# An encoder layer on one core: v from the scaled raw input, its rms applied after the products, its shift added behind attention

## The chip, the core and the metric

The kernel runs on one core of a Trainium2 chip. Its engines work side by side and are ordered by semaphores alone: TensorE (PE, with its weight loads as PEld), VectorE (DVE), ScalarE (ACT), GpSimd (POOL) and SyncE (SP), which issues nearly all transfers. The metric is the time of one execution in microseconds (us); every time below is in us unless it says ns.

## The reference

One layer, 512 tokens of width 1024, all fp32. What matters here:

```python
mod = silu(c) @ w_c + b_c
shift, scl, gate = split(mod, 3)
h = rms_norm(x, g_pre) * (1 + scl) + shift
xa, za, q, k, v, zb, ga, gb = split(h @ w_in, 8)      # 1024 columns each
y_a = ((scan_fwd(conv(xa)) + scan_bwd(conv(xa))) * silu(za)) @ w_pa
y_b = (neighbourhood_attention(q, k, v) * silu(zb)) @ w_pb   # softmax over 8x16 keys, 16 heads of 64
x = x + gate * ((sigmoid(ga) * y_a + sigmoid(gb) * y_b) @ w_o)
out = rms_norm(x, g_final)
```

rms_norm divides a token's row by its root mean square; the softmax weights of one query add up to one.

## The kernel before

Each fp32 product is three fp32r products: an operand is split into a rounded high part and the rest (hi and lo; L380 casts on ACT, L383 subtracts on DVE or GpSimd), and mm3 (L388) adds hi*hi, hi*lo and lo*hi. Width 1024 is 8 blocks k of 128 rows; the normalised input stands transposed, as hh[k] and hl[k], 128 channels by 512 tokens.

The order of every engine's instructions is fixed ahead by a planner (Plan, L101). Each op has an engine or two, a cost, a rank and its data; the planner plays time forward by these costs and gives an engine the op of lowest rank among those that can begin next. HEAD (L44) overrides ranks by name for the start of the kernel. The hardware then runs each engine's list in that order, and an instruction that must wait holds up all behind it on its engine. lock=True marks DVE ops that the planner keeps apart from GpSimd's. SBUF buffers are slots of 512 columns (T, 36 of them) and 1024 columns (W, 32), PSUM is 8 banks of 512 columns given out by class (B, LIMITS). Loads are issued on SP, at most 8 in flight, each waiting for the landing of the one eight before it.

The start runs as follows. par, a table of vectors with c in its first 8 rows, is loaded by ACT's queue (L405). ACT and DVE make silu(c) (L409, L412), TensorE transposes par into prm (L415) and spreads silu(c) over all partitions into two banks cbs (L434 to L440); ACT copies these to SBUF as silr. DVE makes mods from prm (L422). x comes transposed in 8 loads (L474). ACT squares it, DVE adds the squares up, TensorE sums over partitions (L496), ACT and DVE take the root (rstd_ops, L454), TensorE spreads the result over partitions (rb, L509), and ACT copies it (rbs). modulate (L535) makes one column each of scale and shift of block k: DVE multiplies 128x1024 weights wc by silu(c) and sums; for block 0's scale TensorE does it. make_h (L577) is then ht = x * scale * rms on DVE, hh = ht + shift on ACT and hl on DVE. split_v (L604) splits the weights of v.

The first products (vmm, L636) are v: 8 units (2 halves of the columns by 4 tiles of 128 tokens), one bank each, all of them walking over k together, 3 products per unit and block. Stand-in products (fill, L502) keep TensorE running before. vout (L668) copies v to DRAM scratch as hi and lo parts. Then follow 72 projections (proj, L691) of 24 products each, numbered from 9: for each of 4 groups q, k and z of two head pairs, with scores, softmax (attend, L805) and the products with v between the products of the next projections. At the end of attend the gate sz is multiplied by the softmax's reciprocal rcx (L909) and by the head pair's output yt (L911). Then the recurrent branch, the gates, and w_o with the final norm.

## Time and profile before

| | us |
|---|---|
| median of 3 runs (558.74 to 559.42) | 558.84 |
| span of the profiled execution | 556.9 |
| TensorE busy in it | 548.6 (99%) |
| DVE, ACT, GpSimd busy | 388.4, 320.1, 102.1 |

The profile is of one execution; its span runs from the first to the last instruction, and the time of a run has about 2 us more around it. Engine rows give start, duration and shape; an idle time and its releaser stand in brackets where the engine waited. A matmul's duration includes its way through the array, so consecutive ones overlap in the timeline; the chain counts each from the end of the one before.

### The profile page before, as it was taken

What the parts mean: (1) busy time and instruction counts of PE and PEld (TensorE: products, weight loads), DVE (VectorE), ACT (ScalarE), POOL (GpSimd) and SP (SyncE); (2) the same over time, 40 slices, a digit from 0 to 9 for tenths busy, and PEclk for the clock granted to TensorE, in tenths of its full rate; (3) what the DMA queues carried; (4) which work ended last, traced back from release to release, by engine and by line L of the source; (5) the groups of instructions that cost most, each with busy time, mean ns of one, the idle gap of its engine ahead of it and who ended that gap; (6) DMA issues with size and microseconds to landing.
All of it is one profiled execution on the core that took longest, in us unless ns stands there. A gap on an engine that the chain in (4) does not pass through costs nothing.

```text
span 556.9 us, 7643 instructions
## 1 busy us (share of the span) xinstructions
PE 548.6 (99%) x2769; PEld 458.8 (82%) x2769; DVE 388.4 (70%) x707; ACT 320.1 (57%) x557; POOL 102.1 (18%) x98
## 2 busy tenths in 40 slices
PE   8999999999999999999999999999999999999995
PEld 8788888888888888888887888888788888888884
DVE  5999733775775785897458958867968973569423
ACT  6442624763763863766986984996698242223242
POOL 0102757546546520000000000000000000000220
PEclk9999999999999999999999999999999999999998
DMA  8993895651551563035244035131239322480002
GB/s 294 408 408 124 299 302 198 155 191 54 148 202 67 123 200 114 4 95 190 78 123 159 31 122 167 41 114 62 89 100 376 130 76 75 152 301 1 0 38 115
DMA packets 30825, 82.54 MB, mean 148 GB/s; under 512 B 4548, under 2 KB 5700, under 8 KB 30788
## 3 DMA queue, kind: packets, MB, share of 16 engines
q1 hardware_dynamic: 30500, 81.73, 43.3%
q8 instruction: 22, 0.36, 0.3%
q10 hardware_dynamic: 288, 0.33, 0.2%
q14 instruction: 15, 0.12, 0.1%
HBM read 75.60 MB, written 6.44 MB: 147 GB/s over the span
## 4 chain that ended last, share of the span: by engine, by line
PE 99%; DVE 0%; POOL 0%; issue 0%; ACT 0%; POOLq 0%
PE acc L386 79%; PE hx L386 8%; PE pv L386 3%; PE pt L848 2%; PE sp L386 2%; PE gt L386 2%; PE hx L504 1%; PE hx L437 1%; PE hd L551 0%; PE hd L496 0%; PE hd L513 0%; DVE yo L1215 0%; DVE yo L1183 0%; DVE xr L1187 0%; ACT sd L1205 0%
## 5 line engine op out<-in xcount | busy, mean ns | idle before, releaser
L386 PE MATMUL acc<-hhl,whi 128*128 128x512 f32 x784 | 243.1, 391 | 0.0
L386 PEld LDWEIGHTS acc<-hhl,whi 128*128 128x128 f32 x784 | 145.7, 188 | 29.2
L386 PE MATMUL acc<-hhl,wlo 128*128 128x512 f32 x392 | 152.9, 390 | 0.0
L386 PEld LDWEIGHTS acc<-hhl,wlo 128*128 128x128 f32 x392 | 73.6, 188 | 15.5
L380 ACT CAST whi<-wraw 128x1024 fp32r<-128x1024 f32 x72 | 74.4, 1045 | 1.8 <-DMA wraw<-in_w_in_dram 0.9
L1194 POOL TENSOR_TENSOR yo<-yo,gfin 128x512 f32<-128x512 f32 x6 | 8.1, 1350 | 337.8 <-ACT xr L1191 337.7
L383 POOL TENSOR_TENSOR wlo<-wraw,whi 128x1024 fp32r<-128x1024 f32 x23 | 56.0, 2438 | 64.0 <-ACT whi L380 32.1
L383 DVE TENSOR_TENSOR wlo<-wraw,whi 128x1024 fp32r<-128x1024 f32 x49 | 59.2, 1220 | 2.3 <-ACT whi L380 2.1
L386 PE MATMUL acc<-woh,mhl 128*128 128x512 f32 (+1 forms) x144 | 40.4, 366 | 0.0
L386 PE MATMUL acc<-ybhl,whi 128*128 128x512 f32 x128 | 39.4, 390 | 0.0
L386 PE MATMUL acc<-yahl,whi 128*128 128x512 f32 x128 | 39.4, 390 | 0.0
L738 POOL TENSOR_TENSOR nb<-msk,braw 128x192 f32<-128x192 f32 (+1 forms) x48 | 30.7, 670 | 27.8 <-DMA braw<-in_rpb_dram 26.7
L837 ACT ACTIVATE p<-p,mn 128x192 f32<-128x192 f32 (+1 forms) x64 | 30.4, 478 | 6.7 <-DVE mn L830 6.6
L1079 DVE SCALAR_TENSOR_TENSOR gm<-gm,acc 128x512 f32<-128x512 f32 x16 | 11.0, 688 | 33.0 <-PE acc L386 33.0
L386 PE MATMUL hx<-vh,hhl 128*128 128x512 f32 x112 | 33.5, 389 | 0.0
L830 DVE CUSTOM_DVE_ANT_0 p<-sp,nb 128x192 f32<-128x192 f32 (+1 forms) x64 | 31.4, 602 | 0.6 <-PE sp L386 0.2
L386 PEld LDWEIGHTS acc<-woh,mhl 128*128 128x128 f32 x144 | 26.1, 189 | 4.4
L985 DVE SCALAR_TENSOR_TENSOR xc<-acc,prm,xc 128x511 f32<-128x511 f32 (+1 forms) x24 | 18.0, 750 | 14.9 <-ACT xc L978 14.3
L386 PEld LDWEIGHTS acc<-ybhl,whi 128*128 128x128 f32 x128 | 24.0, 188 | 5.0
L386 PEld LDWEIGHTS acc<-yahl,whi 128*128 128x128 f32 x128 | 24.0, 188 | 5.0
L386 PE MATMUL acc<-wol,mhl 128*128 128x512 f32 (+1 forms) x72 | 26.4, 366 | 0.0
L386 PE MATMUL acc<-yahl,wlo 128*128 128x512 f32 x64 | 24.9, 390 | 0.0
(195 smaller groups left out, 939.5 us busy)
## 6 DMA issues: line engine op xcount, KB each, us to landing
wraw<-in_w_in_dram SPq DMA_DIRECT2D x56, 512.0 KB, 5.0
wc<-in_w_m_dram SPq DMA_DIRECT2D x22, 512.0 KB, 10.1
vt<-vscr SPq DMA_DIRECT2D x20, 256.0 KB, 3.5
vscr<-va SPq DMA_DIRECT2D x8, 512.0 KB, 4.3
wraw<-in_w_pb_dram SPq DMA_DIRECT2D x8, 512.0 KB, 3.5
wraw<-in_w_pa_dram SPq DMA_DIRECT2D x8, 512.0 KB
wo<-in_w_o_dram SPq DMA_DIRECT2D x8, 512.0 KB, 5.2
wv<-in_w_v_dram SPq DMA_DIRECT2D x7, 512.0 KB
```

The source lines that it names most:

```text
L380: return lambda e: nc.scalar.copy(o(), i()) if e == "ACT" else nc.vector.tensor_copy(o(), i())
L383: return lambda e: ENGINE[e].tensor_tensor(o(), a(), b().bitcast(F32), op=ALU.subtract)
L386: nc.tensor.matmul(o, a, b, start=first, stop=last)
L437: nc.tensor.matmul(cb.ap[:, k * P:(k + 1) * P], ident.ap[:, 4 * n + k:4 * n + k + 1].to_broadcast([P, P]), par_sb.ap, start=True, stop=True)
L504: op("PE", 0.3, lambda e: nc.tensor.matmul(wb.ap[:, :P], onesc.ap, onesc.ap, start=True, stop=True), 5000 + j, r=[onesc], hold=[wb], until ...
L738: nc.gpsimd.tensor_tensor(o, mv, view, op=ALU.subtract)
L830: nc.vector.tensor_tensor_reduce(out=o, in0=v(spv(h, e)[:, :nk]), in1=v(nb[:, h, :nk]), scale=1.0, scalar=3e38, op0=ALU.add, op1=ALU.min, ...
L837: nc.scalar.activation(pv2(i), pv2(i), AF.Exp, bias=mn.ap[:, c:c + 1], scale=-1.0, accum_out=sm.ap[:, 4 * h + b:4 * h + b + 1])
L848: nc.tensor.transpose(ptp.ap[:, j * P:(j + 1) * P], pt_.ap[:, j * P:(j + 1) * P], ident.ap)
L985: nc.vector.scalar_tensor_tensor(a, b, wcol, a, op0=ALU.mult, op1=ALU.add)
L1079: op("DVE", dve(512), lambda e: nc.vector.scalar_tensor_tensor(t.ap, t.ap, 1.0, o.ap, op0=ALU.add, op1=ALU.mult), n - 1.9, r=[o], rw=[t], ...
L1194: op(("DVE", "POOL"), (dve(w), pool_(w)), lambda e: ENGINE[e].tensor_tensor(y(), y(), gfin[n].ap[:, gs], op=ALU.mult), rank + 0.1, r=[gfin ...
```

## The change

v is linear in h, so v = rms * ((x * scale) @ W_v) + shift @ W_v, and a softmax's weights add up to one, so the second part is a constant per channel that can be added to attention's output. The change uses both:

- hx[k], lx[k]: raw x times the scale of block k, split, made from the first loads; v's products take these. rms multiplies in vout (voh, vol), per token.
- rms comes from x loaded a third time, in token rows (xn), squared with a running sum on ACT; TensorE spreads it (rb) into one bank, ACT copies (rbs).
- Five units of v walk over k together; the other three follow one after the other. At most 6 banks for v; the 2 banks of silu(c) (pair) are read by all modulations directly and given back after silr is copied.
- c is loaded once more by itself (c8), ahead of par; silu(c) is spread from 8 rows. Block 0's scale is made on DVE.
- h for the other projections is made later: ht on GpSimd, shift on ACT (hs), cast (hh) on ACT, hl on DVE. All shift columns (wc*0) are loaded after the rest.
- shift is turned to a row through DRAM and spread (shr); per head pair DVE multiplies the transposed weights of v (w_vt, 8 new loads of 512 KB) by it and sums (cv). L909 and L911 become ytr and yb.
- x and the weights of v come in loads of 512 KB; HEAD has new ranks. The loads of the start, by rank: wc01, x0, wv0, x1, wc11, wc21, wv1, wc31, wv2, wv3, wv4, x2, wv5, wc41, wc51, wv6, wc61, xn1, xn2, x3, wc71, wv7, xn3, xn0, then the shifts; w9 to w15 (projection weights) come in between as their gates open.

```diff
-LIMITS = {"hx": 8, "acc": 3, "sp": 8, "pt": 2, "pv": 2, "mi": 2, "hd": 3, "gt": 8}
+LIMITS = {"cb": 2, "hx": 6, "acc": 3, "sp": 8, "pt": 2, "pv": 2, "mi": 2, "hd": 3, "gt": 8}
...
+    "rn": -24.5555, "sq3": -24.3814, "rd": -24.3812, "sq1": -24.3808, "rbs": -23.8168, "sq0": -23.8167,
+    "sq2": -23.7377, "rr": -23.1868, "rv": -23.1868, "rb": -20.771, "par": -19.6461, "c8": -19.4661,
+    "wc01": -18.9967, "mod011": -18.2714, "x0": -18.0591, "wv0": -18.0187, "x1": -17.8175, "wc11": -17.7222,
+    "cb0": -17.5889, "cb1": -17.5886, "wc21": -17.0274, "wv1": -17.0273, "vl20": -16.9829, "lx5": -16.8171,
+    "vl40": -16.6325, "vl11": -16.2216, "wc31": -16.2215, "vl00": -15.9897, "mod010": -15.9895, "vh00": -15.2342,
+    "wv2": -15.2275, "wv3": -15.2144, "wv4": -15.0849, "vh21": -14.965, "vh31": -14.9648, "hx0": -14.9556,
+    "vh11": -14.9227, "hx1": -14.8864, "vh10": -14.7844, "x2": -14.7206, "vh01": -14.4144, "wv5": -14.1437,
+    "hx2": -14.1283, "wc41": -11.2127, "wc51": -10.9689, "mod10": -10.9101, "lx2": -10.6732, "vl30": -10.6506,
+    "lx3": -10.6502, "lx0": -10.6498, "vl10": -10.6494, "mod41": -10.6491, "mod30": -10.649, "vl61": -10.649,
+    "mod11": -10.6328, "vl21": -10.6163, "wv6": -10.4746, "mod61": -10.4424, "wc61": -9.9113, "xn1": -9.9112,
+    "vol": -9.8476, "xn2": -9.7211, "w9": -9.2629, "voh": -9.1099, "vh50": -9.1099, "vh61": -8.6009,
+    "mod21": -8.5472, "vl41": -8.5331, "vl51": -8.5327, "x3": -8.496, "wc71": -8.4249, "lx1": -8.3181,
+    "vl70": -8.318, "mod51": -8.3178, "vl50": -8.3178, "vl71": -8.3176, "vl31": -8.2434, "hx6": -8.2376,
+    "vl60": -7.9836, "vh40": -7.456, "hx4": -7.3237, "mod20": -7.1116, "vh20": -6.9125, "hx7": -6.9125,
+    "sht": -6.8405, "vl01": -6.8401, "lx4": -6.6641, "lx7": -6.664, "hx3": -6.547, "vh41": -6.5466, "hx5": -6.5327,
+    "vh51": -6.5326, "vh71": -6.449, "vh60": -6.4007, "mod71": -6.1288, "mod00": -6.1285, "wv7": -5.9891,
+    "vh30": -5.87, "vh70": -5.6813, "xn3": -5.5188, "lx6": -4.8536, "w10": -4.518, "mod31": -4.4195, "xn0": -4.3793,
+    "wc60": -3.8783, "wc30": -3.7292, "wc40": -3.5764, "wc50": -3.1556, "wc10": -3.0913, "wc20": -2.8982,
+    "wc00": -2.1309, "w11": -1.8085, "wc70": -1.3694, "wlo10": 3.5288, "ht0": 4.0245, "hs3": 4.37, "ht6": 4.3831,
+    "ht1": 4.5527, "ht2": 4.5848, "wlo11": 4.5852, "ht5": 4.9249, "whi9": 4.9984, "ht7": 5.2332, "ht3": 5.3297,
+    "ht4": 5.3298, "hh3": 5.3561, "hh2": 5.3603, "hh1": 5.473, "hs5": 5.4732, "hh4": 5.4799, "silr": 5.5365,
...
+}
+AFTER = []
...
+    def bank(i, cls):
+        if cls == "cb":
+            assert i not in plain
+            twin.append(i)
+            return pair[:, 512 * len(twin) - 512:512 * len(twin)]
+        if i not in twin:
+            plain.add(i)
+            return ps.tile([P, 512], F32, tag=f"b{i}", name=nm(cls))
+        if not rest:
+            first.close()
+            rest.append(ctx.enter_context(tc.tile_pool(name="pr", bufs=1, space=bass.MemoryType.PSUM)))
+        return rest[0].tile([P, 512], F32, tag=f"b{i}", name=nm(cls))
+
...
+    tan8, c8 = const("tan8", [8, P]), const("c8", [8, P])
+    op("ACT", 0.45, lambda e: nc.scalar.dma_start(c8.ap, par[:8, :]), -41, w=[c8], late=2.6, name="c8")
+    op("ACT", 0.45, lambda e: nc.scalar.dma_start(par_sb.ap, par), -40, w=[par_sb], late=3.3, name="par")
+    op("ACT", 0.3, lambda e: nc.scalar.activation(tan8.ap, c8.ap, AF.Tanh, scale=0.5), -25, r=[c8], w=[tan8])
+    op("DVE", 0.3, lambda e: nc.vector.scalar_tensor_tensor(c8.ap, tan8.ap, 1.0, c8.ap, op0=ALU.add, op1=ALU.mult),
+       -22, r=[tan8], rw=[c8])
...
+    cbs = [B("cb") for _ in range(2)]
+        def f(e, n=n):
+                nc.tensor.matmul(cbs[n].ap[:, k * P:(k + 1) * P], ident.ap[:8, 4 * n + k:4 * n + k + 1].to_broadcast([8, P]), c8.ap,
+        op("PE", 0.6, f, -21 + n, r=[ident, c8], w=[cbs[n]], name=f"cb{n}")
...
+    for j in range(4):
+        load(xT[j], whole(xT[j]), x_t[j], -19.9 + 0.1 * j, 524288, spare=2, name=f"x{j}")
+    ssx, rxc = const("ssx", [P, NT]), const("rxc", [P, NT])
+    for t in range(NT):
+        xn = W("xn")
+        load(xn, whole(xn), x[t * P:(t + 1) * P, :], 0, 524288, spare=2, name=f"xn{t}")
+        op("ACT", act(1024, 0, True), lambda e, xn=xn, t=t: nc.scalar.activation(xn.ap, xn.ap, AF.Square, accum_out=ssx.ap[:, t:t + 1]), 0,
+           rw=[xn], w=[ssx], name=f"sq{t}")
...
+    op("ACT", 0.29, lambda e: nc.scalar.activation(rsd.ap, ssx.ap, AF.Sqrt, bias=epsc.ap), 0, r=[ssx, epsc], w=[rsd], name="rd")
+    op("DVE", 0.17, lambda e: nc.vector.tensor_scalar(rv.ap, ssx.ap, D * EPS, None, op0=ALU.add), 0, r=[ssx], w=[rv], name="rv")
+    op("DVE", 0.17, lambda e: nc.vector.reciprocal(rrc.ap, rsd.ap), 0, r=[rsd], w=[rrc], name="rr")
+    op("DVE", 0.57, newton, 0, r=[rrc, rv], w=[rq, rxc], lock=True, name="rn")
...
+    rb, rbs = B("mi"), T("rbs")
+    def spread(e):
+        for t in range(NT):
+            nc.tensor.matmul(rb.ap[:, t * P:(t + 1) * P], rxc.ap[:, t:t + 1].to_broadcast([P, P]), ident.ap, start=True, stop=True)
+    op("PE", 0.5, spread, -12, r=[rxc, ident], w=[rb], name="rb")
+    spread_done = op("ACT", act(512), cast(whole(rbs), whole(rb)), -12, r=[rb], w=[rbs], name="rbs")
...
+    def modulate(k, m):
+        t, r = W("wc"), C("sc", 1, 10) if m else shc.part(k, k + 1)
+        (scs if m else shs)[k] = r
+        b = mods.ap[:, 8 + k:9 + k] if m else pc(16 + k, 17 + k)
+        g = mods.ap[:, k:k + 1] if m else 0.5
+        load(t, whole(t), w_m[3 * k + m], k - 5, 524288, spare=2, name=f"wc{k}{m}")
...
+                op("DVE", dve(512) + 0.08, lambda e, j=j, z=z: nc.vector.tensor_tensor_reduce(
+                    out=t.ap[:, z], in0=t.ap[:, z], in1=cbs[j].ap, scale=g, scalar=a.ap if j else b, op0=ALU.mult, op1=ALU.add,
+                    accum_out=r.ap if j else a.ap), -0.5, r=[cbs[j], mods, prm] + [a] * j, rw=[t], w=[r if j else a], name=f"mod{k}{m}{j}")
+            return
+        op("DVE", dve(1024) + 0.08, lambda e: nc.vector.tensor_tensor_reduce(
+            out=t.ap, in0=t.ap, in1=pair, scale=g, scalar=b, op0=ALU.mult, op1=ALU.add, accum_out=r.ap),
+           k - 1.5, r=cbs + [mods, prm], rw=[t], w=[r], after=[zero], name=f"mod{k}{m}")
+    def split_x(k):
+        hx[k], lx[k] = two("xhl")
+        xk = lambda: xT[k // 2].ap[:, k % 2 * 512:k % 2 * 512 + 512]
+        op("ACT", act(512, 1), lambda e: nc.scalar.activation(hx[k].ap, xk(), AF.Copy, scale=scs[k].ap), k - 1.19,
+           r=[xT[k // 2], scs[k]], w=[hx[k]], name=f"hx{k}")
+        op("DVE", dve(512) + 0.06, lambda e: nc.vector.scalar_tensor_tensor(
+            lx[k].ap, xk(), scs[k].ap, hx[k].ap.bitcast(F32), op0=ALU.mult, op1=ALU.subtract), k - 1.18,
+           r=[xT[k // 2], hx[k], scs[k]], w=[lx[k]], lock=True, name=f"lx{k}")
...
+        xk = lambda: xT[k // 2].ap[:, k % 2 * 512:k % 2 * 512 + 512]
+        op("POOL", pool_(512), lambda e: nc.gpsimd.tensor_tensor(t.ap, xk(), rbs.ap, op=ALU.mult), k - 1.2, r=[xT[k // 2], rbs], w=[t], name=f"ht{k}")
+        op("ACT", act(512, 2), lambda e: nc.scalar.activation(t.ap, t.ap, AF.Identity, scale=scs[k].ap, bias=shs[k].ap), k - 1.195,
+           r=[scs[k], shs[k]], rw=[t], name=f"hs{k}")
+        op("ACT", act(512), cast(whole(hh[k]), whole(t)), k - 1.19, r=[t], w=[hh[k]], name=f"hh{k}")
+        op("DVE", dve(512), sub(whole(hl[k]), whole(t), whole(hh[k])), k - 1.18, r=[t, hh[k]], w=[hl[k]], lock=True, wait=1.45, name=f"hl{k}")
...
+        t, z = W("wv"), (slice(0, S), slice(S, D))
+        load(t, whole(t), w_v[k], k - 4.5, 524288, spare=2, name=f"wv{k}")
+        (h0, l0), h1, l1 = two("vhl"), T("vh", F32R), T("vl", F32R)
+        for n, hi, lo in ((0, h0, l0), (1, h1, l1)):
+            vh[k, n], vl[k, n] = (hi, whole(hi)), (lo, whole(lo))
+            op("ACT", act(512), lambda e, hi=hi, n=n: nc.scalar.copy(hi.ap, t.ap[:, z[n]]), k - 1.1, r=[t], w=[hi], name=f"vh{k}{n}")
+            op(*(("POOL", pool_(512)) if k and n else (("DVE", "POOL"), (dve(512), pool_(512)))), sub(whole(lo), lambda n=n: t.ap[:, z[n]], whole(hi)), k - 1.09, r=[t, hi],
+               w=[lo], lock=True, name=f"vl{k}{n}")
...
+        modulate(k, 1)
+        split_x(k)
+        split_v(k)
+    for k in range(KD):
+        modulate(k, 0)
+    silr = W("silr")
+    op("ACT", act(1024), cast(whole(silr), lambda: pair), 9, r=cbs, w=[silr], name="silr")
...
+        for j, parts in enumerate(([0], [1], [2]) if k < 2 else ([0, 1], [2]) if k < KD - 1 else ([0, 1, 2],)):
+            for m, u in enumerate(VU[:5]):
+                ops.append(vmm(u, k, parts, k + 0.1 * j + 0.01 * m))
+            fill(ops[4], vps[VU[4]])
+    for m, u in enumerate(VU[5:]):
+        ops = [vmm(u, k, [0, 1, 2], 8 + 0.2 * m + 0.01 * k) for k in range(KD)]
...
+        rs = rxc.ap[:, t:t + 1]
+        op("ACT", act(512, 1), lambda e: nc.scalar.activation(view(0, 192), src(), AF.Copy, scale=rs), rank, r=[vps[u], rxc], w=[a], name="voh")
+        def low(e):
+            for b in range(2):
+                o, i1 = (a.ap.rearrange("p (g c) -> p g c", g=4)[:, :, c:c + 64] for c in (64 + 64 * b, 192 * b))
+                nc.vector.scalar_tensor_tensor(o, src()[:, :, b, :], rs, i1.bitcast(F32), op0=ALU.mult, op1=ALU.subtract)
+        op("DVE", 2 * dve(256), low, rank, r=[vps[u], rxc], rw=[a], name="vol")
...
+    sscr = pl.fixed(dp.tile([32, P], F32, name="sscr"))
+    op("DVE", 0.2, lambda e: nc.vector.transpose(sht.ap[:, :32], shc.ap), 7, r=[shc], w=[sht], name="sht")
+    op("SP", 0.5, lambda e: nc.sync.dma_start(turned(sscr.ap), sht.ap[:, :32]), 8, r=[sht], w=[sscr], size=16384, late=SLACK, name="shs")
+    shr = W("shr")
+    load(shr, whole(shr), bass.AP(sscr.ap.tensor, sscr.ap.offset, [[0, P], [1, D]]), 8, 524288, r=[sscr], spare=3, name="shr")
...
+    def v_bias(pr, rank, after):
+        t = W("wvt")
+        load(t, whole(t), w_vt[pr], rank - 2, 524288, after=after, spare=5, name="wvt")
+        op("DVE", dve(1024) + 0.08, lambda e: nc.vector.tensor_tensor_reduce(
+            out=t.ap, in0=t.ap, in1=shr.ap, scale=0.5, scalar=0.0, op0=ALU.mult, op1=ALU.add, accum_out=cvs[pr].ap), rank,
+           r=[shr], rw=[t], w=[cvs[pr]], lock=True, name="cv")
...
-        op("DVE", dve(512), lambda e: nc.vector.tensor_tensor(rbc(sz.ap), rbc(sz.ap), nat(rcx.ap), op=ALU.mult),
-           pos - 0.3, r=[rcx], rw=[sz], lock=True, name="szr")
-        op("DVE", dve(512), lambda e: nc.vector.tensor_tensor(rbc(sz.ap), nat(yt.ap), rbc(sz.ap), op=ALU.mult), pos + 0.5, r=[yt],
-           rw=[sz], lock=True, name="yb")
+        v_bias(pr, pos + 0.2, gate_of(len(main), 2))
+        op("DVE", dve(512), lambda e: nc.vector.tensor_tensor(rbc(rct.ap), nat(yt.ap), nat(rcx.ap), op=ALU.mult),
+           pos + 0.4, r=[yt, rcx], rw=[rct], lock=True, name="ytr")
+        op("DVE", dve(512), lambda e: nc.vector.scalar_tensor_tensor(sz.ap, rct.ap, cvs[pr].ap, sz.ap, op0=ALU.add, op1=ALU.mult),
+           pos + 0.5, r=[rct, cvs[pr]], rw=[sz], lock=True, name="yb")
```

## Rows read from the trace of the kernel before

**Rows 1.** Page, chain that ended last: share of the span by engine.

```profile
PE 99%; DVE 0%; POOL 0%; issue 0%; ACT 0%; POOLq 0%
```

**Rows 2.** That chain in order of time: start us, us, engine, tile, line, count.

```profile
1.51 3.36 PE hx L504 x14
...
5.09 2.99 PE hx L437 x16
8.08 2.46 PE hx L504 x22
...
16.34 44.23 PE hx L386 x192
60.57 32.64 PE acc L386 x144
...
550.14 0.43 DVE yo L1183
```

**Rows 3.** Timeline of DVE, 0 to 62 us: start us, us, instruction [idle before].

```profile
4.29 0.28 DVE L412 SCALAR_TENSOR_TENSOR par_sb<-tan,par_sb 8x128 f32<-8x128 f32 x1 [4.29 <-ACT tan L409]
...
5.86 0.17 DVE L425 TENSOR_SCALAR mods<-mods 128x8 f32<-128x8 f32 x1
...
14.89 0.16 DVE L462 SCALAR_TENSOR_TENSOR rx<-q,r 128x2 f32<-128x2 f32 x1
14.99 0.48 DVE L584 SCALAR_TENSOR_TENSOR ht<-xT,sc,hd 128x256 f32<-128x256 f32 x1
...
17.92 0.81 DVE L566 CUSTOM_DVE_ANT_0 wc<-wc,hx,mods 128x512 f32<-128x512 f32 x1 [0.31 <-DMA wc<-in_w_m_dram]
...
24.51 1.34 DVE L571 CUSTOM_DVE_ANT_0 wc<-wc,silr,mods 128x1024 f32<-128x1024 f32 x1
...
37.68 0.75 DVE L600 SCALAR_TENSOR_TENSOR hhl<-ht,sh,hhl 128x512 fp32r<-128x512 f32 x1
...
53.70 1.21 DVE L383 TENSOR_TENSOR wlo<-wraw,whi 128x1024 fp32r<-128x1024 f32 x1
```

**Rows 4.** Timeline of ACT, 0 to 62 us.

```profile
3.94 0.31 ACT L409 ACTIVATE tan<-par_sb 8x128 f32<-8x128 f32 x1 [1.26 <-DMA par_sb<-in_par_dram]
...
16.65 0.62 ACT L380 CAST vh<-wv 128x512 fp32r<-128x512 f32 x1 [0.37 <-DMA wv<-in_w_v_dram]
...
20.75 0.72 ACT L598 ACTIVATE hhl<-ht,sh 128x512 fp32r<-128x512 f32 x1 [0.40 <-DVE ht L595]
...
40.69 1.05 ACT L380 CAST vh<-wv 128x1024 fp32r<-128x1024 f32 x1 [0.17 <-DMA wv<-in_w_v_dram]
```

**Rows 5.** One xT load, issue to landing; DMA rate, 8 to 12 us.

```profile
L375 SPq DMA_DIRECT2D xT<-in_x_t_dram x1: 432/432/432, 2.1 to 2.1; - x1
DMA to landing us min/median/max: 4.6/4.6/4.6
GB/s 389 287 123 143 266 143 143 143 205 143 123 164 205 266 307 266 348 266 369 287 389 410 369 369 389 430 410 389 348 492 389 410 328 492 410 410 430 471 430 451
```

**Rows 6.** Stretches: length, busy PE, PEld, DVE, ACT, POOL; clock, DMA share, GB/s.

```profile
30.00:35.00 5.00, 5.00 (x23) 4.14 (x22) 5.00 (x8) 1.44 (x2) 0.00 (x0) 1.00 1.03 408
120.00:140.00 20.00, 20.00 (x127) 16.84 (x126) 11.81 (x26) 8.31 (x15) 11.93 (x10) 1.00 0.38 129
240.00:260.00 20.00, 20.00 (x109) 16.97 (x109) 17.98 (x35) 11.27 (x24) 0.00 (x0) 1.00 0.45 141
```

**Rows 7.** Timeline of POOL (GpSimd), 0 to 62 us.

```profile
15.38 1.28 POOL L383 TENSOR_TENSOR vl<-wv,vh 128x512 fp32r<-128x512 f32 x1 [13.83 <-ACT vh L380]
...
53.81 3.35 POOL L383 TENSOR_TENSOR wlo<-wraw,whi 128x1024 fp32r<-128x1024 f32 x1 [7.32 <-DVE hhl L600]
```

**Rows 8.** One tile's, one line's instructions: duration ns min/median/max, first and last start us.

```profile
L383 POOL TENSOR_TENSOR wlo<-wraw,whi x23: 2378/2396/3352, 53.8 to 197.9; 128x1024 fp32r<-128x1024 f32 x23
L909 DVE TENSOR_TENSOR sz<-sz,rcx x8: 650/687/1903, 115.9 to 260.8; 128x512 f32<-128x512 f32 x8
```

## Prediction

> **What bounds the kernel now.** I read the shares of the chain first, then the chain in order of time, then each engine's rows in the first 62 us. The chain is 99% TensorE [rows 1]. In order of time it has three parts [rows 2]: a start up to 16.34 us in which TensorE runs stand-ins (L504) and small helpers (L437 and others) but no product of the layer; then products without a gap, the 192 of v first (44.23 us), until 550.14; then a tail of DVE, ACT and one store to 556.9. So the middle costs its matmuls whatever the other engines do, and three things can move the time: when the first v product begins, what TensorE must wait for afterwards, and matmuls added. The profiled span is 556.9; the median of the runs is 558.84, so 1.9 lies around it. I work in the span and add 1.9.

> Why 16.34? DVE's rows end in the rms of x: the last Newton step (rx) ends at 15.05, and ht, which multiplies by its spread, at 15.47 [rows 3]. The first v product needs ht, then hh. What else it needs was there much earlier: the modulation's constants at 6.03 [rows 3].

> **Part by part.** (1) *The start.* The rms leaves the way to the first product; what is left on it is silu(c), the scale of block 0 and hx0. c8 is a small load; I let it land where par does, at 3.94, when ACT's tanh starts [rows 4]. Tanh 0.31 [rows 4] and DVE's product 0.28 [rows 3] give 4.6. TensorE is then still in stand-ins: the code's list plans each at 0.3 and by its own costs puts 8 before cb0 (7 before par's transpose now). Two entries each, 0.24 an entry (3.36/14 [rows 2]): until 5.35. An entry takes 0.24 at first and 0.112 later (2.46/22); the 16 of silu(c) took 2.99, which puts the step near 7.3 [rows 2], and I keep it there. Then 17 entries (cb0, transpose, cb1; with 8 rows of c instead of 128 I charge the same, as no row shows 8) end at 8.3, the transpose at 7.3. Transpose to constants is 0.94 (5.09 to 6.03 [rows 2, 3]): 8.2. The two halves of the scale, 0.81 each [rows 3], end at 9.8; wc01 has landed long before. hx0 is one 128x512 ACT pass with an operand per partition, 0.72 [rows 4]: 10.5. TensorE has 12 planned stand-ins after cb1, 24 entries at 0.112: 11.0. Both say about 10.85, against 16.34: **-5.5**. Bounds: -6.5 (entries of 8 rows at half the price; then the constants' chain ends at 9.6), -4.2 (c8 queued behind x, 1.3 later).

> (2) *The v stage.* TensorE's need: 5 units by 3 products by 0.227 (32.64/144 [rows 2]) is 3.4 us a block k, where eight units made 5.44. In the order of the new ranks, what blocks 0 to 7 wait for are the 3rd, 7th, 9th, 10th, 14th, 15th, 20th and 22nd loads of half a megabyte. The fourth 256 KB of x, issued at 2.1, lands 4.6 later [rows 5], so the second half megabyte is there at 6.7; then one each 1.28 (0.524 MB at 408 GB/s [rows 6]). That gives wv1 13.1, wc41 22.1, x3 29.7, wc71 31.0. Behind wc lie 1.34 (its product on DVE [rows 3]) and 0.72 (hx); behind wv 0.62 (vh [rows 4]). Blocks are wanted at 10.85 + 3.4k: k=1 at 14.25 (ready 13.7), k=4 at 24.4 (ready 24.2), k=6 at 31.2 (ready 30.4), k=7 at 34.6 (ready 33.1). Nothing waits, by 0.2 at the closest. But by the same count the 27th half megabyte of today would be there at 38.7, and ACT gets it at 40.69 [rows 4]; part of that is a hole from 8.2 to 9.3, where most slices show 123 to 266 GB/s [rows 5], with eight small transfers under way and no more; the new ones are twice as large. So waits of 0 to 2.3; I take 0.7, which is also what today's v stage loses (44.23 less 192 x 0.227). **0**, bounds -0.7 and +1.6. DVE carries per block 1.34 + 0.75 (lx) + about 0.7 (vl) = 2.8 of 3.4; ACT 2 of 3.4, and four squarings of 1.1 to 1.3 in all.

> (3) *rb* now sits among the products: 8 entries at 0.112. **+0.9**, bounds 0.5 (if entries of rb overlap the products around them) and 1.0.

> (4) *Hand-over to the projections.* v ends at about 10.85 + 43.5 + 0.9 + 0.7 = 56. From there block k is wanted at 56 + 0.68k, with ht (GpSimd), hs and hh (ACT), hl (DVE) behind it. xn0 is the 25th or 26th half megabyte: 36 to 37.4; its squaring 1.3, rstd 1.2: 40. All eight banks are then taken (2 by silu(c), 6 by v), so rb waits for unit 0 to be copied out: 0.62 on ACT and two DVE passes of 0.48 [rows 3, 4]: 41.6; spread and copy 1.5: 43. ht is 1.28 by GpSimd's 128x512 row [rows 7]: eight are 10.3, and with wlo11 (2.40 [rows 8]) between them 55.7; the last (k=4 by the ranks) has hs and hh behind it, 1.35: 57.1, wanted at 58.7. The shift products end with wc70, about the 34th load: 47.7 plus 1.34. It fits by 1.6. DVE from 39 on: eight shift products 10.7, hl 6, four units' copies 4, wlo9 1.2 and rstd 1 are 23 of 20 us, so copies slip behind v's end, where DVE is free today from 54.9 [rows 3]. I take **+0.4**, bounds 0 and +4, for GpSimd and DVE get in each other's way: GpSimd's wlo took 3.35 when DVE's wlo ran from 53.70 [rows 3, 7], 2.40 as a rule [rows 8], so a DVE subtraction of 1.21 cost it 0.95.

> [...]

> (5) *Behind attention.* Per pair one load of 512 KB and one DVE reduction more (1.34 by its shape [rows 3]); L909 and L911 become two of the same size. That is 8 x 1.34 = 10.7 on DVE and 4.7 MB of loads with shr; the links are at 129 to 141 of 408 GB/s there [rows 6]. From 120 to 140 DVE is busy for 11.8 of 20, but from 240 to 260 for 17.98 [rows 6]. cv is queued on DVE ahead of score minima and evictions that TensorE waits for; its own waits are for wvt and for GpSimd. L909 shows the second: 0.69 as a rule, 1.90 once [rows 8]. TensorE has no gap there today, so no row shows its slack; the list asks for wvt two projections (10.9 us) ahead. **0**, bounds 0 (nothing is taken from TensorE here, so no gain) and +2.

> Sum: -5.5 + 0 + 0.9 + 0.4 + 0 = **-4.2**: span 552.7, time 554.6.

> **The rivals.** *Data paces v.* The loads run 2 late, as today's count did; blocks from 4 on wait 2.3 in place of 0.7: 556.2, and 556.8 with the rms behind the same loads. For: the hole and the 40.69; against: larger transfers. *GpSimd late at the hand-over.* Its queue of 12.7 (ht, wlo11) meets 6 us of DVE's two-input work after 43; losing 0.95 of every 1.21, its last ht ends near 60.4 instead of 55.7, hh at 61.8, and TensorE waits 3.1 more: 557.7, up to 558.6 with wlo10 in between as well. For: the 3.35 row; against: the eight shift products, the largest part of DVE, read PSUM in the new form. *cv stops attention (slower).* If cv stands in DVE's queue waiting for wvt or GpSimd, the minima and evictions behind it come late. With 8 pairs it decides from 0.5 us a pair, which eats the 4.2; at 1.0 a pair, less than L909's one delay of 1.2, the time is 562.6. For: that 1.90, and 17.98 of 20; against: 8.2 of 20 idle from 120 to 140, and L909's delays cost TensorE nothing. *The start does not move*, as hx0 waits for something that I missed: 559; no row speaks for it.

> **How the numbers follow.** A measurement here tells 0.2%, 1.1 us. Forecast 0.62 (552.6 to 556.2), data 0.14 (faster), GpSimd 0.11 (0.05 faster, 0.06 within), attention 0.09 (slower), start 0.04 (0.03 within, 0.01 slower). Faster 0.81, same 0.09, slower 0.10. The range takes in the data case and GpSimd's cheaper half: 552.6 to 557.7; outside stay the slower rival, the worst hand-over and the last of the bounds added up.

> **What would show it.** First product on hx near 10.8; no TensorE wait above 0.5 before block 4; v's last product near 56; rb a single piece of 0.9 around 42; ht of 1.3 on GpSimd, longer where DVE's subtractions run; projections without a gap from there; DVE from 240 to 260 above 19 of 20. A first product at 12 or later, DVE waiting for wvt in front of the minima, or idle TensorE after 60 makes it wrong.

## The result, and the profile after

The changed kernel takes 561.34 us (median of 4 runs, 561.06 to 562.92) where the kernel before, run beside it, takes 558.93: a ratio of 1.0050, 95% interval 1.0035 to 1.0064. It is slower, by 2.4 us. The forecast was 554.6 with a range to 557.7; it missed by 6.7 us, and the time moved the other way. The profiled executions say the same: span 559.3 against 556.9.

The page of the changed kernel, TensorE's total and the shares of the chain that ended last, where [rows 1] gave TensorE 99%:

```profile
PE 546.6 (98%) x2725; PEld 455.1 (81%) x2725; DVE 410.5 (73%) x715; ACT 329.7 (59%) x575; POOL 127.9 (23%) x114
...
PE 92%; DVE 5%; DMA 2%; issue 1%; ACT 1%; ACTq 0%
```

DVE now holds 5% of the chain. Which waits of TensorE that is, the view of waits says (columns: engine, tile, line, what it waited for; us in total, times, longest):

```profile
PE acc L411 <- DVE hhl L408: 3.1, 1, 3.1
PE hx L513 <- POOL onesc L429: 1.5, 1, 1.5
PE hx L411 <- DVE vhl L408: 1.4, 1, 1.4
```

The 1.5 is the first stand-in's and was there before. The 1.4 lies in the v stage ("the wait near 24" below), the 3.1 at the hand-over from v to the projections. They stand in TensorE's own timeline, with the first v product (start us, us, instruction, count, idle before it and its releaser; pieces of three stretches):

```profile
10.98 1.59 PE L411 MATMUL hx<-vhl,xhl 128*128 128x512 f32 x4
...
25.17 1.21 PE L411 MATMUL hx<-vhl,xhl 128*128 128x512 f32 x4 [1.44 <-DVE vhl L408]
...
72.91 0.50 PE L411 MATMUL acc<-hhl,whi 128*128 128x512 f32 x1 [3.10 <-DVE hhl L408]
```

By stage, from the starts of the first product of each (before, then after): first v product 16.10 and 10.98, -5.1; v stage to the first projection 44.3 and 47.0, +2.7; from there to the first scores of pair 0 32.7 and 38.3, +5.6; from the scores to the last matmul 457.0 and 456.6, -0.4; tail 6.8 and 6.4, -0.4. The sum is +2.4. So the start gave about what it should, and two stages took it back, with 2.4 on top.

Both waits end in one DVE instruction that took far longer than its kind. DVE around the first (start us, us, instruction), and GpSimd in the same stretch:

```profile
14.56 0.75 DVE L550 SCALAR_TENSOR_TENSOR xhl<-xT,sc,xhl 128x512 fp32r<-128x512 f32 x1
...
16.48 1.78 DVE L550 SCALAR_TENSOR_TENSOR xhl<-xT,sc,xhl 128x512 fp32r<-128x512 f32 x1
18.19 3.49 DVE L408 TENSOR_TENSOR vhl<-wv,vhl 128x512 fp32r<-128x512 f32 x2
...
23.36 1.75 DVE L408 TENSOR_TENSOR vhl<-wv,vhl 128x512 fp32r<-128x512 f32 x1
```
```profile
14.73 1.74 POOL L408 TENSOR_TENSOR vl<-wv,vh 128x512 fp32r<-128x512 f32 x1 [13.11 <-ACT vh L572]
16.42 1.29 POOL L408 TENSOR_TENSOR vhl<-wv,vhl 128x512 fp32r<-128x512 f32 x1
17.68 3.46 POOL L408 TENSOR_TENSOR vl<-wv,vh 128x512 fp32r<-128x512 f32 x2
```

An lx takes 0.75 at 14.56, just ahead of GpSimd's vl, and 1.78 at 16.48, just behind the start of one. The vl at 23.36 is the one that ends the wait. DVE and GpSimd around the second wait (wlo is the low part of a projection's weights, nb a piece of attention's bias, subtracted from a mask):

```profile
65.31 1.27 DVE L540 CUSTOM_DVE_ANT_0 wc<-wc,pair,prm 128x1024 f32<-128x1024 f32 x1
...
66.75 6.11 DVE L408 TENSOR_TENSOR hhl<-ht,hhl 128x512 fp32r<-128x512 f32 x2
```
```profile
65.96 2.41 POOL L408 TENSOR_TENSOR wlo<-wraw,whi 128x1024 fp32r<-128x1024 f32 x1
68.33 3.38 POOL L685 TENSOR_TENSOR nb<-msk,braw 128x256 f32<-128x256 f32 x6
```

Of the 6.11 the first hl has 5.51: it begins while wlo runs, and the six nb behind wlo all pass it. The second, after GpSimd's last nb, has 0.68. The shift product ahead of them, which reads one operand from PSUM, keeps its 1.27 though wlo starts within it. TensorE is idle from 69.8 to 72.9, and the four microseconds behind the idle stretch run at a granted clock of 0.57, 11 matmuls instead of the 19 of the next four (stretch, length, busy time of each engine, granted clock, DMA share, GB/s):

```profile
69.70:73.00 3.30, 0.20 (x2) 0.09 (x1) 3.30 (x4) 0.66 (x2) 2.01 (x4) 1.00 1.00 269
73.00:77.00 4.00, 4.00 (x11) 3.14 (x12) 3.60 (x8) 1.72 (x3) 2.79 (x2) 0.57 1.01 399
```

### The profile page after: what moved, and what is told of

Its sections match the earlier page's. It is cut to its first block, busy times and chain, and to the rows that moved or that the text cites. A ratio compares the mean times of both kernels' runs of the same rounds, so it can differ in the third digit from the quotient of the medians.

```text
span 559.3 us, 7626 instructions
## 1 busy us (share of the span) xinstructions
PE 546.6 (98%) x2725; PEld 455.1 (81%) x2725; DVE 410.5 (73%) x715; ACT 329.7 (59%) x575; POOL 127.9 (23%) x114
## 4 chain that ended last, share of the span: by engine, by line
PE 92%; DVE 5%; DMA 2%; issue 1%; ACT 1%; ACTq 0%
PE acc L411 77%; PE hx L411 5%; PE pv L411 3%; PE pt L811 2%; PE sp L411 2%; PE gt L411 2%; DVE hhl L408 1%; DMA wraw<-in_w_in_dram 1%; DVE wc L540 1%; DVE vhl L408 1%; DVE xhl L550 1%; DMA c<-in_par_dram 1%; PE pair L460 0%; PE mi L506 0%; DVE va L629 0%
## 5 line engine op out<-in xcount | busy, mean ns | idle before, releaser
L800 ACT ACTIVATE p<-p,mn 128x192 f32<-128x192 f32 (+1 forms) x64 | 30.4, 477 | 6.7 <-DVE mn L793 6.6
L685 POOL TENSOR_TENSOR nb<-msk,braw 128x192 f32<-128x192 f32 (+1 forms) x48 | 34.1, 745 | 0.0
L411 PE MATMUL hx<-vhl,xhl 128*128 128x512 f32 x96 | 24.8, 399 | 1.4 <-DVE vhl L408 1.4
L411 PE MATMUL acc<-ybhl,wlo 128*128 128x512 f32 x64 | 24.9, 389 | 0.0
```

Source lines behind the costliest of these rows:

```text
L411: nc.tensor.matmul(o, a, b, start=first, stop=last)
L685: nc.gpsimd.tensor_tensor(o, mv, view, op=ALU.subtract)
L800: nc.scalar.activation(pv2(i), pv2(i), AF.Exp, bias=mn.ap[:, c:c + 1], scale=-1.0, accum_out=sm.ap[:, 4 * h + b:4 * h + b + 1])
```

## Experiments

The theory, called port in the expectations: a GpSimd instruction holds up a DVE one that reads two SBUF operands (lx at 1.78 for 0.75, vl at 1.75, hl at 5.51 for 0.68), and that makes both waits. What the two engines share there, no run shows; what the runs show is who met whom and how long each took. The fills below only write, and what they stand for is left out of the layer. Rivals: DVE's list puts hl and the shift products too late whatever GpSimd does; the loads are late.

### GpSimd's share of the conflict taken out

```diff
-                    nc.gpsimd.tensor_tensor(o, mv, view, op=ALU.subtract)
+                    nc.gpsimd.memset(o, 0.0) if pr < 2 else nc.gpsimd.tensor_tensor(o, mv, view, op=ALU.subtract)
```

> The changed kernel with GpSimd's twelve bias subtractions of pairs 0 and 1 (nb, two SBUF inputs) replaced by a fill of the same tiles, in the same places of every engine's list; the relative position bias of those two pairs is left out. Theory (GpSimd's instructions hold up a DVE one that reads two SBUF tiles): the hl that took 5.51 us from 66.75 waits for wlo alone, ends by 69.2, TensorE's wait of 3.10 falls below 0.5 and the slow products behind it go with it: 556.3 to 558.3. Rival 1 (DVE's list puts the shift products and hl too late, GpSimd has nothing to do with it): hl ends near 72, 560.8 to 561.8. Rival 2 (loads late): the same 561.

Measured 556.32, ratio to before 0.9952 (0.9933 to 0.9970). The hl in question, with the one behind it, and GpSimd:

```profile
65.69 2.55 DVE L408 TENSOR_TENSOR hhl<-ht,hhl 128x512 fp32r<-128x512 f32 x2
```
```profile
64.68 2.42 POOL L408 TENSOR_TENSOR wlo<-wraw,whi 128x1024 fp32r<-128x1024 f32 x1 [2.73 <-issue]
67.03 1.36 POOL L685 MEMSET nb<- 128x256 f32 x6
```

The first waits for wlo alone and ends at 67.6, the second runs beside fills in 0.68, and TensorE has no wait at the hand-over. With every engine's list the same, order and loads are out as causes of the 3.1. Part of the gain beyond the hand-over was not expected: the wait near 24 was 0.3 in this run. One lx makes that difference. First the changed kernel, then this run, DVE and GpSimd:

```profile
21.60 1.83 DVE L550 SCALAR_TENSOR_TENSOR xhl<-xT,sc,xhl 128x512 fp32r<-128x512 f32 x1
21.60 1.29 POOL L408 TENSOR_TENSOR vl<-wv,vh 128x512 fp32r<-128x512 f32 x1 [0.47 <-ACT vh L572]
```
```profile
21.69 0.74 DVE L550 SCALAR_TENSOR_TENSOR xhl<-xT,sc,xhl 128x512 fp32r<-128x512 f32 x1
21.76 1.83 POOL L408 TENSOR_TENSOR vl<-wv,vh 128x512 fp32r<-128x512 f32 x1 [0.54 <-ACT vh L572]
```

Here DVE begins 0.07 ahead, and GpSimd pays instead.

```diff
-sub(whole(lo), lambda n=n: t.ap[:, z[n]], whole(hi))
+lambda e, ...: nc.gpsimd.memset(lo.ap.bitcast(F32), 0.0) if e == "POOL" else sub(...)(e)
```

> The changed kernel with those low parts of W_v (vl) that GpSimd subtracts replaced by a fill, in the same places of every list; so the low part of W_v is missing in them. Theory (GpSimd's subtraction holds DVE's up): lx and vl on DVE between 16 and 25 fall from 1.75-1.83 to 0.70-0.75, the 1.44 wait at 23.7 is gone, v ends 1.4 to 2.0 earlier (56.0 to 56.6 against 58.0). The time falls by that only if the hand-over lets it: the hl that ends at 72.3 is paced by GpSimd's own list, so the wait there may grow by as much: 559.3 to 561.3. Rival (v is paced by its loads or by the order of DVE's list): the wait at 23.7 stays, 561.3.

Measured 558.93, ratio 1.0014 (0.9998 to 1.0029): no different from the kernel before, and better than expected. DVE between 16 and 21:

```profile
16.46 0.75 DVE L550 SCALAR_TENSOR_TENSOR xhl<-xT,sc,xhl 128x512 fp32r<-128x512 f32 x1
17.12 0.69 DVE L408 TENSOR_TENSOR vhl<-wv,vhl 128x512 fp32r<-128x512 f32 x1
18.48 0.69 DVE L408 TENSOR_TENSOR vhl<-wv,vhl 128x512 fp32r<-128x512 f32 x1 [0.67 <-ACT vhl L572]
```

All at 0.7; the wait near 24 is gone and the first projection starts at 55.5 instead of 58.0. Of these 2.5, 0.8 is there at the fifth product already, as the clock did not fall at the start of this execution (see the next section). The hand-over did not take that back: its hl again lasts 5.50, from 64.20, since GpSimd's list moved forward with it.

The third run has both of these edits in one kernel, nb of pairs 0 and 1 and GpSimd's vl as fills.

> The two edits together (bias of pairs 0 and 1 filled, GpSimd's vl filled; both left out of the result). Theory (port): both waits gone, 1.5 to 2 from v and 3 to 5 from the hand-over: 554.3 to 556.8, below the kernel before by 2 to 4. If they only hide each other, no better than the first of the two alone, 556.3 to 558.3. Rivals (order, loads): 561.

Measured 555.10, ratio 0.9932 (0.9913 to 0.9951). So the conflict between the two engines costs the changed kernel about 6 us, of which some 0.5 is the start's clock, which did not fall in this execution either; without it the change is worth 4 against the kernel before, which is the forecast's sum.

### The first products and the clock

```diff
-nc.tensor.matmul(..., ident.ap[:8, 4 * n + k:4 * n + k + 1].to_broadcast([8, P]), c8.ap, ...)
+nc.tensor.matmul(..., ident.ap[:, 4 * n + k:4 * n + k + 1].to_broadcast([P, P]), cf.ap, ...)   # cf: c8 and 120 rows of zeros
```

> The changed kernel with silu(c) spread by products over 128 rows (8 of c and 120 of zeros) in place of 8 rows; the same 16 entries at the same place. Theory (what TensorE did in those entries holds the granted clock down: 0.81, 0.50 and 0.56 in 7.6-9, 9-11 and 11-12): the granted clock is 1.00 from 7.6 on or soon after, entries come every 0.112 from there, the first v product comes at 10.6 to 11.2 and the first spacings are 0.23 in place of 0.57 and 0.40: 560.6 to 561.2. Rival (the pause before 5.55 or something else sets the clock): the clock stays at 0.5, 16 entries at 0.21 take 1.6 longer, the first v product at 12 to 12.6: 562.3 to 563.

Measured 560.64, ratio 1.0031 (1.0018 to 1.0044), which overlaps with the changed kernel's. The windows, first of the changed kernel, then of this one (the granted clock is the third number from the end):

```profile
7.60:9.00 1.40, 1.40 (x11) 1.40 (x12) 1.33 (x3) 0.00 (x0) 0.00 (x0) 0.81 1.04 421
9.00:11.00 2.00, 2.00 (x12) 2.00 (x11) 1.21 (x4) 1.66 (x4) 0.00 (x0) 0.50 1.03 420
```
```profile
7.60:9.00 1.40, 1.40 (x15) 1.40 (x14) 1.07 (x3) 0.00 (x0) 0.00 (x0) 1.00 1.02 416
9.00:11.00 2.00, 1.21 (x11) 1.02 (x11) 1.21 (x3) 1.40 (x3) 0.00 (x0) 1.00 1.03 420
```

With 128 rows the clock stays at 1.00, the first product starts at 10.88 and the fifth at 11.93 instead of 12.41, as the theory has it. But one execution of each does not settle it. In four other profiled executions with the 8-row products the clock stays at 1.00 as well: bias filled, vl filled, both filled, and the shift products moved up (below). The first of them:

```profile
7.60:9.00 1.40, 1.40 (x13) 1.38 (x13) 1.24 (x3) 0.00 (x0) 0.00 (x0) 1.00 1.02 389
```

In two more (below: cv left out; bias and decay moved) it falls to 0.50 as in the changed kernel, and in none of the five with 128 rows does it fall. So 8 rows alone do not bring the clock down; that they have a part in it is suggested and not shown, and what else decides stays open. The 0.5 does not last: after short delays from 15 on TensorE comes to the wait near 24 at 24.03 (23.72 in the changed kernel) and leaves it at 25.37 (25.17), when DVE's vl ends: DVE sets that moment.

### GpSimd's bias moved

```diff
-            nbs.append(bias(pr, n0 + BD * (1 - pr % 2), gate_of(n0, 2) if pr else [main[6]]))
+            nb = bias(pr, n0 + BD * (1 - pr % 2), gate_of(n0, 2) if pr else [main[6]])
+            nbs.append(nb if pr < 2 else nb([]))
...
+        if g == 0:
+            nbs = [nb([main[12]], 12.5) for nb in nbs]
```

The bias of pairs 0 and 1 is loaded as before and subtracted later, from the start of the fourth projection on.

> The changed kernel, complete, with GpSimd's twelve bias subtractions of pairs 0 and 1 moved in its list from around the hand-over (60 to 72) to behind the weight split of the fifth projection, so after 72; their first reader is DVE's score minimum near 92. Theory (port): as with the bias filled, the hl that took 5.51 us waits for one wlo alone and the wait of 3.10 goes: 555.8 to 557.2, faster than the kernel before by 0.3 to 0.55%. What could eat it: the twelve subtractions now lie beside DVE's ql, kl and rms-free small steps between 72 and 82, where TensorE has work queued. Rival (order of DVE's list): 560.5 to 561.5.

Measured 562.36, ratio 1.0068 (1.0056 to 1.0080): a miss. The wait of 3.1 at the hand-over is gone as expected, and 2.8 of idle TensorE stands around the first scores instead, 94 to 99, most of it for DVE's sz (attention's gate):

```profile
PE sp L411 <- DVE sz L859: 2.4, 2, 1.9
```

With a granted clock of 0.57 from 99 to 103 behind it, the scores to the last matmul take 5.6 longer than in the changed kernel. DVE, where the 26 small steps of decay now meet GpSimd:

```profile
71.67 0.17 DVE L895 TENSOR_TENSOR lt<-lt,lt 128x16 f32<-128x16 f32 x1
...
72.30 2.30 DVE L899 TENSOR_TENSOR lt<-lt,lt 128x16 f32<-128x16 f32 x1
74.63 2.33 DVE L900 TENSOR_SCALAR lt<-lt 128x16 f32<-128x16 f32 x1
76.99 0.61 DVE L899 TENSOR_TENSOR lt<-lt,lt 128x16 f32<-128x16 f32 x1
```
```profile
72.16 4.76 POOL L408 TENSOR_TENSOR wlo<-wraw,whi 128x1024 fp32r<-128x1024 f32 x2 [2.49 <-ACT whi L405]
76.88 2.39 POOL L688 TENSOR_TENSOR nb<-msk,braw 128x256 f32<-128x256 f32 x4
```

A step of 0.17 takes one GpSimd instruction each: 2.3 beside a weight split, 0.5 to 0.6 beside a bias subtraction. DVE is busy with them to 94, so the scores' sz and kl come late. The expectation named these steps as a neighbour and did not price them. The profiled execution is the slowest of the five and starts late besides, its first v product at 13.46: the 16 products over 8 rows and the stand-ins behind them come one each 0.21 up to there.

The next run has cf with its 128 rows in place of c8, as above, on top of the bias moved.

> The same with silu(c) spread over 128 rows as well, complete. In the run of that edit alone the first stretch of v gained 0.5 and the time 0.7, part of it lost again in the wait at the hand-over; without that wait the 0.5 should come through: 555.2 to 556.7, 0.3 to 0.7 below the run with the later bias alone. If the wait of 1.4 near 24 (GpSimd's vl) takes it back, no difference.

561.91, ratio 1.0054 (1.0040 to 1.0068): 5 above the range, as the wait before the scores stands again (2.7). It is 0.45 below the run before, but the intervals overlap, so this does not tell whether the start's 0.5 comes through.

```diff
-"mod50": 7.6499, "mod40": 7.8313, "mod60": 8.2301
+"mod50": 5.3, "mod40": 5.31, "mod60": 5.32
```

> The changed kernel, complete, with three shift products (mod50, mod40, mod60) moved up in DVE's list, ahead of hl; GpSimd keeps the bias where it was in its list. Rival (order of DVE's list): with the products out of the way hl comes in time, the wait at 69.6 goes: 556 to 558. Theory (port): hl is held up by whatever GpSimd runs beside it; the bias subtractions or a wlo still stand beside the six hl at the end, single ones of them take 2 us and more, TensorE still waits 2 or more in all: 559 to 562.

563.76, ratio 1.0084 (1.0071 to 1.0097), slower than either expected; TensorE waits 2.2 for hh and 2.8 for hl between 58 and 64. It is no clean test of order, because the planner drew up DVE's whole list anew and hl came behind copies of v that end with v itself. What it does show is the same hl beside the same nb in another pattern:

```profile
63.59 4.07 DVE L408 TENSOR_TENSOR hhl<-ht,hhl 128x512 fp32r<-128x512 f32 x4
```
```profile
61.99 6.10 POOL L685 TENSOR_TENSOR nb<-msk,braw 128x256 f32<-128x256 f32 x6
```

Both engines take 1.02 an instruction here, turn by turn, instead of one being passed six times. And right behind, in the same run, stands the longest hold-up of all, a step of decay that takes 0.17 alone, with GpSimd beside it:

```profile
69.02 13.06 DVE L892 TENSOR_TENSOR lt<-lt,lt 128x16 f32<-128x16 f32 x1
```
```profile
69.21 2.38 POOL L408 TENSOR_TENSOR wlo<-wraw,whi 128x1024 fp32r<-128x1024 f32 x1
71.56 3.42 POOL L685 TENSOR_TENSOR nb<-msk,braw 128x256 f32<-128x256 f32 x6
74.95 7.10 POOL L408 TENSOR_TENSOR wlo<-wraw,whi 128x1024 fp32r<-128x1024 f32 x3
```

It begins before the wlo, is passed by ten GpSimd instructions, and ends when their unbroken run does. TensorE did not wait for it.

### What attention adds

```diff
-        op("DVE", dve(1024) + 0.08, lambda e: nc.vector.tensor_tensor_reduce(out=t.ap, in0=t.ap, in1=shr.ap, ...
+        op("DVE", dve(1024) + 0.08, lambda e: nc.vector.memset(cvs[pr].ap, 0.0), rank,
```

> The changed kernel with DVE's product for the shift of v (cv, eight of 1.34 us) replaced by a fill of the eight columns; the shift's part of v is left out, the loads of the transposed W_v stay. If cv costs nothing behind attention, as the traces say (scores to end 456.5 against 456.9): within 0.3 of the changed kernel, 561.0 to 561.7. If it costs in hidden places (DVE is full from 240 to 260): 559 to 560.5.

561.96, ratio 1.0059 (1.0044 to 1.0074), 0.3 above the range for no cost: nothing gained. From the first scores to the last matmul TensorE takes 456.6 in both kernels, so cv is free there.

### Towards a kernel that keeps the two apart

```diff
-    small(9, [main[8]])
+    small(33, [main[32]])
```

The steps of decay come behind the four groups of attention; the bias is moved as above.

> The changed kernel, complete, with two things moved: the bias of pairs 0 and 1 behind the fifth projection's weight split, as in the run before, and DVE's 26 small steps of the gates' decay (128x16 each) from 68-94 to behind the last projection of attention, where GpSimd has nothing to do. Theory (port): in the run with the bias alone moved, the small steps took 0.49 to 2.33 each in place of 0.17, one GpSimd instruction each, DVE was full to 94 and TensorE waited 4.0 before the scores of pair 0; with the small steps gone that wait is gone too: 555.8 to 557.3. Rival (ql, kl, sz and cv alone, 6.6 us of DVE's work, are held up by the twelve subtractions and three weight splits from 72 to 92 as well): the scores still wait 1 to 3: 557.5 to 560.

558.02, ratio 0.9990 (0.9978 to 1.0002), 4.3 less than without the second edit; 0.7 above the theory's range and inside the rival's. The wait before the scores is down from 2.8 to 0.4, less than the rival's 1 to 3, and what is left of it is DVE's cv, ahead of sz and the score minima in its list. DVE and GpSimd:

```profile
86.53 0.69 DVE L742 SCALAR_TENSOR_TENSOR kl<-acc,kh 128x512 fp32r<-128x512 f32 x1 [4.76 <-ACT kh L741]
87.14 5.16 DVE L726 CUSTOM_DVE_ANT_0 wvt<-wvt,shr 128x1024 f32<-128x1024 f32 x1
...
92.23 1.22 DVE L726 CUSTOM_DVE_ANT_0 wvt<-wvt,shr 128x1024 f32<-128x1024 f32 x1
```
```profile
85.43 3.43 POOL L688 TENSOR_TENSOR nb<-msk,braw 128x256 f32<-128x256 f32 x6
88.82 2.40 POOL L408 TENSOR_TENSOR wlo<-wraw,whi 128x1024 fp32r<-128x1024 f32 x1
```

kl (the low part of k) reads PSUM and SBUF and keeps its 0.69; cv reads two SBUF tiles and takes 5.16, beside the third nb, which runs when it begins, and passed by the last three and the wlo; then 1.22 alone. From the scores to the last matmul this run takes 2.0 more than the changed kernel. The wait is 0.4 of it; the rest is not placed, and TensorE's own list there is another one.

Then cf with its 128 rows on top of bias and decay moved.

> The same with silu(c) spread over 128 rows, complete. Theory (8-row products cost the start 0.5 through the clock): 0.4 to 0.7 below the run without it, 555.2 to 556.8. Rival (the wait near 24, GpSimd's vl, is set by its own chain and takes the 0.5 back): the same as without it.

558.03, ratio 0.9984 (0.9976 to 0.9993): the rival. The wait near 24 ends at 25.22, with 8 rows at 25.20. On top of this, three vl moved to DVE and block 3 of W_v split ahead of block 4:

```diff
-"vh30": -5.87, "vl40": -16.6325
+"vh30": -7.4565, "vl40": -10.6495
-sub(whole(lo), ...)
+lambda e, ...: sub(whole(lo), ...)("DVE" if (k, n) in ((4, 1), (5, 0), (5, 1)) else e)
```

> The same, complete, with the low parts vl41, vl50 and vl51 on DVE in place of GpSimd (0.69 each there, against 1.05 that a GpSimd one costs a DVE instruction beside it) and W_v's block 3 split ahead of its block 4, so that vl30 stands before vl40 on DVE. Theory (port): DVE's lx3 and vl30 take 0.7, the wait of 1.1 to 1.4 near 24 goes: 1.0 to 1.6 below the run without, 553.8 to 555.8. Rival (DVE is simply full between 14 and 35, or W_v's loads are late): the wait moves to a later block, no more than 0.5 gained.

558.04, ratio 0.9980 (0.9971 to 0.9989): by its time the rival again, a wait moved to a later block. Its cause is still the conflict: the wait near 24 is gone, and one of 0.8 stands at 28.4, for an lx that takes 1.78 beside one of the vl that stayed on GpSimd.

The last run moves what was planned in other places only where it is written out:

```diff
+    # written out in another place than planned
+    def hold(self, o):
+        if o.name == "nb":
+            self.nbs += 1
+            return "n1" if self.nbs <= 12 else "n2" if self.nbs <= 18 else None
+        if o.name == "decay":
+            self.dec += 1
+            return f"d{self.dec}"
+        return None
...
+        if o.name == "wlo15":
+            return ["n1"]
...
-            sub(whole(lo), ...)
+            sub(whole(lo), ...)("DVE" if (k, n) in ((3, 1), (4, 1), (5, 0), (5, 1), (6, 1)) else e)
-        sub(whole(low), whole(raw), whole(hi))
+        lambda e: sub(whole(low), whole(raw), whole(hi))("DVE" if n in (11, 12) else e)
```

The first pair of changed lines is vl, the second wlo; cf with 128 rows and block 3 of W_v ahead of block 4 are in it as well.

> The changed kernel, complete, with TensorE's list as it was in the run with silu(c) over 128 rows, and GpSimd and DVE kept apart: the bias of pairs 0 and 1 behind GpSimd's weight split of the seventh projection, that of pair 2 four splits later; the weight splits of the third and fourth projection on DVE; the 13 double steps of decay spread over DVE's steps after 220, where GpSimd is idle; five more low parts of W_v (vl31, 41, 50, 51, 61) on DVE, and W_v's block 3 split ahead of block 4. Theory (port): no wait of TensorE above 0.5 anywhere between the first v product and the end; against the changed kernel 0.5 from the start, 1.4 near 24, 0.3 and 3.1 and 1.9 at the hand-over, in all 7: 553.8 to 555.6, as the run with both parts filled. Rival (DVE full from 12 to 36 with 3.5 us more of its own): the wait near 24 moves to a later block, 555.6 to 557.

555.31, ratio 0.9935 (0.9921 to 0.9949): 3.9 below the kernel before and 6 below the changed one. TensorE's waits, complete:

```profile
PE hx L546 <- POOL onesc L461: 1.5, 1, 1.5
PE hx L443 <- ACT vhl L605: 0.8, 1, 0.8
PE pv L443 <- DVE rc L893: 0.2, 1, 0.2
```

The 0.8 is the start's own chain, ahead of the first product. By stage against the kernel before: start -5.3, v +1.3, hand-over 0.0, and 0.6 more behind it. Several edits were made at once here, so the run says that they suffice, not what each is worth.

## Why the prediction was wrong, point by point

*What bounds the kernel, and the start.* Right. The first product came at 10.98 where 10.85 was forecast, against 16.10 and not the 16.34 of the chain [rows 2]: -5.1. That it came so close is partly luck, as the times between were off and cancelled: c8 went out second and landed at 4.9 instead of 3.9, the 16 entries of 8 rows began at 5.55 and took 1.9, as the step to the faster rate was kept. Not foreseen was the step back: the products of the next microsecond cost 0.57 and 0.40, 0.5 in all. Charging 8 rows like 128 was harmless for the entries themselves; whether it was what slowed the products behind them, the runs do not show.

*The v stage with rb, 0.9 forecast, 2.7 measured.* rb was right, 0.89 for 0.9 (43.64). 1.4 is the wait near 24, and the 0.4 that is left about the slow start. Loads were not the cause, although the rival of late data had the larger chance: filling vl alone removed the wait. The step that failed is "DVE carries per block 1.34 + 0.75 (lx) + about 0.7 (vl) = 2.8 of 3.4". lx and vl took 1.75 to 1.83 five times in a row from 16.48 on; the durations were taken from rows in which GpSimd was idle. Before, GpSimd has two vl, one nb at 45.42 and no other subtraction until the wlo at 53.81 [rows 7]; the change gives it nine vl from 14.73 on, and the prediction never laid them beside DVE's. That one nb was a warning, in rows that neither the prediction nor [rows 3, 7] has: DVE's ht beside it took 1.16, the others 0.75.

```profile
45.42 1.07 POOL L738 TENSOR_TENSOR nb<-msk,braw 128x256 f32<-128x256 f32 x1 [26.65 <-DMA braw<-in_rpb_dram]
```
```profile
45.88 1.16 DVE L595 SCALAR_TENSOR_TENSOR ht<-xT,sc,rbs 128x512 f32<-128x512 f32 x1
```

*The hand-over, 0.4 forecast, 5.6 measured.* This is the main error, and the step that failed is the price of that term: the mechanism was named, that GpSimd and DVE get in each other's way, but it was priced on GpSimd alone. One row, wlo at 3.35 beside a DVE subtraction of 1.21 that started 0.11 earlier [rows 3, 7], was read as "a DVE subtraction costs GpSimd 0.95", and so the rival watched GpSimd's ht. Those ran at 1.26 each, eight in 10.09 from 45.23 on, and ended at 55.3 where 55.7 was forecast. DVE lost instead: 2.2 beside wlo at 58.2, 4.8 at 66.75, where hl waited for a wlo and was passed by six nb. The nb were in no term at all. What the prediction set against that rival, that the shift products read PSUM, no row of before showed to matter; in the changed kernel the one at 65.31 kept its 1.27 with a wlo beginning within it. The bound of +4 was for a late ht; the true price is 3.1 of idle, 1.8 of slow clock behind the idle stretch (eight matmuls of 0.227 fewer), and 0.7 more, of which 0.3 at 61 and 0.2 at 65 stand right behind an hl each. The planner did not prevent it, although lx, vl, hl and cv have lock=True: it keeps them apart from GpSimd's in its own count of time, only the order of each list reaches the chip, and there they met.

In the single meetings seen here the one that began later lost: wlo 0.95 when DVE had started 0.11 ahead [rows 3, 7], and lx 1.03 when vl had (1.78 for 0.75, at 16.48). Beside fills, hl kept its 0.68. In GpSimd's unbroken runs the order of beginning did not decide: hl at 66.75 was passed by six nb that began after it (5.51 for 0.68), and the step at 69.02, which began 0.19 ahead of GpSimd's run, was held for all of it (13.06 for 0.17). The prediction used one direction, DVE ahead of GpSimd, in these two stages; the other, L909's 1.90 on DVE [rows 8], it kept for cv.

*Attention, 0 forecast.* Right in this kernel: scores to last matmul took 0.4 less than before, and leaving cv's work out gained nothing. DVE is busy 19.15 of 20 from 240 to 260, as foreseen, at no cost. The slower rival, cv held up by GpSimd, has a real mechanism all the same: 5.16 in the run with bias and decay moved, worth 0.4 of waiting to TensorE.

*The chances.* Slower had 0.10, 0.09 of it on cv in attention and 0.01 on the start. The mechanism that came true was in the list, as "GpSimd late at the hand-over", with an upper price of 558.6 and a sign that stayed below the kernel before. With DVE as the loser, the same overlap gives 5.51 for one hl, and no bound of the text reached that. Of its own signs of being wrong one came true, idle TensorE after 60. The sum without the conflict was sound: 555.1 with both parts filled, 555.3 with the two kept apart, 554.6 forecast. Part of that closeness is luck: with both filled the hand-over cost 1.3 for 0.4, and the stages behind it gave 0.8 for 0.

*Left open.* Why hl at 66.75, cv at 87.14 and the step at 69.02 were passed by six, four and ten GpSimd instructions, each to the end of an unbroken run, while six hl in a row took turns with six nb. Whether the order alone, with GpSimd idle, would have cost anything beyond the 1.0 of idle that the run with both parts filled shows at 58, beside its wlo.

## What to carry to other kernels

Work moved to GpSimd, or moved next to it, cost this kernel most on DVE's instructions whose operands all stand in SBUF (lx 1.78 for 0.75, hl 5.51 for 0.68). So lay both timelines side by side, and charge each meeting in both directions (wlo lost 0.95, lx 1.03), up to the length of GpSimd's whole unbroken run (13.06 for a step of 0.17 beside ten instructions). DVE's instructions with a PSUM operand were the ones that could stand beside GpSimd (a shift product kept 1.27, kl 0.69); short steps without one cost most for their length there, one GpSimd instruction each (2.30 and 2.33 for 0.17 beside a weight split, 0.49 to 0.62 beside a bias subtraction). When a duration is taken from a row, look at what the neighbour did in that row: ht took 1.16 beside an nb, 0.75 without.
